# The forget gates' chain ahead of the value casts, and two NSA output tiles that take the last pair of heads behind the others, in a two-layer hybrid attention trunk

## The chip, the cores and the metric

The kernel runs on one core of one Trainium2 chip. The metric is the device time of one execution in microseconds (us). The engines are TensorE (PE; its weight loads are shown as PEld), VectorE (DVE), ScalarE (ACT), GpSimd (POOL) and SyncE (SP, which here only issues transfers). Each engine runs its own list of instructions in order; semaphores hold an instruction until what it reads has been written and what it overwrites has been read.

## The reference: what is computed

The input is x, 512 tokens by 1024 channels, float32. Each of two layers computes, cut to what matters here:

```python
h = rmsnorm(x, norm_mix)
q_a, k_a, v_a, f_a, q_b, kv_b, g_b, gate_a, gate_b = split(h @ w_in)
log_f = log_sigmoid(f_a + b_forget)                  # 8 forgetting heads (FoX)
c = cumsum(log_f)                                    # over the tokens
s = q_a @ k_a.T / 8 + c[:, None] - c[None, :]        # causal
y_a = (softmax(s) @ v_a) @ w_o_fox
# NSA: 8 query heads, 2 key/value heads; three branches
# (compressed, selected, sliding window) with partial rotary embedding
o_n = g[..., 0:1]*o_c + g[..., 1:2]*o_s + g[..., 2:3]*o_w     # g = sigmoid(g_b)
y_b = o_n @ w_o_nsa
mixed = sigmoid(gate_a)*y_a + sigmoid(gate_b)*y_b
x = x + mixed @ w_out
x = x + square(relu(rmsnorm(x, norm_mlp) @ w_up)) @ w_down
```

A final rmsnorm follows the second layer. The forget chain makes c, a running sum of the logarithms of the forget gates. At the end of the attention the change touches o_n and its product with w_o_nsa.

## The kernel before, in words

The whole trunk is one stream of work on one core. The state is held with channels on the partitions and the 512 tokens along the free axis. A float32 product is made from rounded pieces: each operand is split into a high part (fp32r) and the remainder, and for every block of 128 channels PE runs three matmuls of 512 columns: high by high (L243), high weight by low data (L244), low weight by high data (L245). The weights arrive as raw float32 by a transfer on SP (L201); `convert` rounds them on ACT (L217, tile wh) and subtracts on DVE (L218, tile wl). There are two buffers each for raw, wh and wl, and a raw buffer is free for the next load when the split has read it.

The order of every engine's instructions is not the source order alone: the kernel is written against a scheduler that places each instruction of a whole stage by its readiness and priority, so a small edit of the source can move instructions elsewhere on several engines. The source's order still says which result an instruction needs and which buffer it takes.

A layer (`Body.layer`) goes through these steps:

- `token_proj` makes the FoX values, four blocks of 128 tokens, in the PSUM banks S, S, PT, PT. `rstd` makes the reciprocal norm: rc, with one column for each block of tokens, and R, the same spread over the partitions.
- A second `token_proj` of 288 columns makes, for each block b, g2[b]: 256 columns of NSA values, 8 of the forget gates, 24 of NSA's branch gates. They lie in the banks mm, mm, O, O. Its matmuls are the lines L357 to L359.
- For each block the kernel then makes z (forget logits, DVE L884), th (tanh of the branch gates, ACT L886), and the high and low part of the NSA values VN (ACT L887, DVE L888). The gates follow (DVE L891, L893).
- CRS, the table of cosines and sines for the rotary embedding, is loaded (L895, on SP, 512 KB) and multiplied by R in two instructions on POOL (L897). It is one tile for both layers.
- `forget` (L783 to L808) turns the 128x32 logits into log sigmoid by a chain of small instructions, one on ACT (L789, exp) and the others on DVE (L788 to L799, among them a polynomial in six steps, L796). Ten matmuls of 128 columns (L805, L806) then make the running sum over the tokens in bank S.
- The projections of q, k and the gates (`block`, one bank and 24 matmuls each), FoX attention, NSA attention. Both attentions have the same shape on the engines: scores on PE, exp on ACT, a reciprocal and normalization on DVE (FoX L449 and L454, NSA L562 and L566), transposes on PE (FoX L464, NSA L579), casts and splits of those, products with the values.
- The end of each NSA pair of heads (`after`, four of them in a layer): four matmuls for the compressed branch (L962), then for each half of the 128 output rows a copy out of PSUM (ACT L969) and an addition (DVE L970), and the split into oh and ol (`out_pair`, ACT L495, DVE L496).
- The output projection of NSA, eight tiles m, two for each 128x1024 weight tile w. `half(1, m, w)` runs twelve matmuls: for each of the four pairs k (the entries of yb) the three kinds L243, L244, L245. The last pair's oh and ol are the newest data they need. Then the gate is applied (DVE L1039, L1040), and `mix` splits the sum (L1030, L1031) for w_out. The MLP follows.

PSUM has eight banks of 128x512; a tag such as "mm" or "S" names a pair of banks that take turns, so a matmul that begins a new tile waits until the bank's last reader is done.

Of the kernel before, what the change touches and what calls it, by code (L numbers as in the profile page):

```python
# [14 lines left out]
OP = mybir.AluOpType  # L15
# [4 lines left out]
T = 512  # L20
KT = D // 128
NB = T // 128
# [10 lines left out]
OFF, N_SMALL = {}, 0  # L33
# [104 lines left out]
def run(*gens):  # L138
    for g in gens:
        for _ in g:  # L140
            pass


class Body:
# [705 lines left out]
    def layer(self, l, u):  # L850
        nc, a = self.nc, self.a
# [10 lines left out]
        R, rc = self.rstd(self.acc, ("O", "O"), wait=g, R=self.R)  # L862
        run(g)
        small = self.small
        g2 = [self.p(t) for t in ("mm", "mm", "O", "O")]
        g = self.token_proj([[a["wg2"][l, c].rearrange("p j m -> p (j m)")] for c in range(4)], 288, g2, u)
        VF = []
        for b in range(NB):
# [4 lines left out]
                                           op0=OP.mult, op1=OP.subtract)  # L873
# [2 lines left out]
        VN = self.t("vn", [128, NB, 4, 128], F32R)  # L876
        z = self.t("z", [128, NB, 8])
        th = self.t("th", [128, NB, 24])
        rch = self.t("s4", [128, NB], name="rch")
        nc.vector.tensor_scalar(rch, rc, 0.5, None, op0=OP.mult)  # L880
        for b in range(NB):
            pv = g2[b][:, :256].rearrange("p (h d) -> p h d", h=4)
            r = rc[:, b:b + 1]
            nc.vector.scalar_tensor_tensor(z[:, b], g2[b][:, 256:264], r, small[:, OFF["bf"]:OFF["bf"] + 8],  # L884
                                           op0=OP.mult, op1=OP.add)
            nc.scalar.activation(th[:, b], g2[b][:, 264:288], AF.Tanh, scale=rch[:, b:b + 1])  # L886
            nc.scalar.activation(VN[:, b, :, :64], pv, AF.Copy, scale=r)  # L887
            nc.vector.scalar_tensor_tensor(VN[:, b, :, 64:], pv, r, VN[:, b, :, :64].bitcast(F32),  # L888
                                           op0=OP.mult, op1=OP.subtract)
        self.gates = gt = self.t("gates", [128, NB, 3, 8])  # L890
        nc.vector.tensor_scalar(gt, th.rearrange("p b (h c) -> p b c h", c=3), 0.5, 0.5, op0=OP.mult, op1=OP.add)  # L891
        for b in range(NB):
            nc.vector.tensor_scalar(gt[:, b, 0], gt[:, b, 0], self.const("rowv")[:, b:b + 1], None, op0=OP.mult)  # L893
        self.CRS = self.t("crs", [128, 2, T])
        nc.sync.dma_start(self.CRS, a["rope"])  # L895
        for i in range(2):
            nc.gpsimd.tensor_tensor(self.CRS[:, i], self.CRS[:, i], R, op=OP.mult)  # L897
        self.forget(z.rearrange("p b h -> p (b h)"))

        st, hl = {}, []  # L900

# [52 lines left out]
        def nsa_pair(p):  # L954

            hk = p // 2
            O = [None]

            def after(O):
                for e in range(2):  # L960
                    for bank in range(2):
                        nc.tensor.matmul(O[:, bank, e], self.vz[:, hk, e],  # L962
                                         self.pc[hk][p % 2][:, bank * 256:(bank + 1) * 256], start=False, stop=e == 1)
                o = self.t("zz", [128, T], name="o")
                t = self.t("tmp", [128, T])
                half = lambda x: x.rearrange("p (b c) -> p b c", b=2)
                for e in range(2):
                    s, f = slice(64 * e, 64 * e + 64), slice(64 * (1 - e), 64 * (1 - e) + 64)
                    nc.scalar.copy(half(t[s]), O[f, :, e])  # L969
                    nc.vector.tensor_add(half(o[s]), O[s, :, e], half(t[s]))  # L970
                st["ob", p] = self.out_pair(o)

            ready = (lambda: ("qb", p) in st and "ks" in st and "kw" in st, lambda: hk in self.pc)

            def unit(br, e):
                return dict(br=br, e=e, p=p, hk=hk, O=O, after=after, ready=ready[br], kk=lambda: KK[hk],
                            q=lambda: st["qb", p][:, e], v=lambda b: VN[:, b, 2 * br + hk],
                            gate=lambda: gt[:, :, 1 + br, 2 * p + e],
                            steps=(self.pair_scores, self.pair_transposes, self.pair_values))
            u = [unit(br, e) for br in range(2) for e in range(2)]  # L980
            for i in range(4):
                u[i]["other"], u[i]["second"] = u[(i + 2) % 4], u[i | 1]
            return u

        def half(kind, m, w):

            xs = ya if kind == 0 else yb
            ps = self.p("mm")
            yield from self.gemm(ps, w, 4 * (m % 2), xs, ks=4)
            st["y"] = ps  # L990
# [30 lines left out]
        yb = [st["ob", p] for p in range(4)]  # L1021
# [4 lines left out]
        def mix():  # L1026
            y = MA[len(mixed) // 2][:, len(mixed) % 2]
            h = self.t("oh", [128, T], F32R)
            lo = self.t("ol", [128, T], F32R)
            nc.scalar.activation(h, y, AF.Copy, scale=0.5)  # L1030
            nc.vector.scalar_tensor_tensor(lo, y, 0.5, h.bitcast(F32), op0=OP.mult, op1=OP.subtract)  # L1031
            mixed.append((h, lo))

        for m in range(8):
            if m % 2 == 0:
                w = self.weights(a["wo"][l, 1, m // 2].rearrange("p i c -> p (i c)"))
            run(half(1, m, w))
            t, y = st["gb", m], MA[m // 2][:, m % 2]
            nc.vector.scalar_tensor_tensor(t, t, 1.0, st["y"], op0=OP.add, op1=OP.mult)  # L1039
            nc.vector.tensor_add(y, y, t)  # L1040
            if m % 2:
                mix()
# [9 lines left out]
        for m in range(8):  # L1052
            ps = self.bank()
            w = self.weights(a["wout"][l, m].rearrange("p k c -> p (k c)"))
# [439 lines left out]
```

## Time and profile before

| | |
|---|---|
| median of three runs | 1522.34 us (1522.2 to 1523.99) |
| the profiled execution | 1523.61 us, of which the profile's span is 1521.8 us |
| granted clock of PE, mean | 0.997 |
| PE busy | 1507.1 us, 99% of the span |
| DVE, ACT, POOL busy | 1097.7, 810.0, 191.1 us |
| transfers | 188.81 MB, 124 GB/s over the span |

A row of the timeline reads: start in us, length in us, engine and line, operation, output<-inputs with the tile names of the program, shape, how many instructions the row stands for, and in brackets the idle time of that engine just before, with what ended it. The length is from the start of an instruction until its result is there; a matmul of 512 columns has a length of 0.39, but the next can start sooner, since PE is a pipeline. A row with x2 or x4 stands for several neighbours. SPq marks the issuing of a transfer, not the transfer. The list of waits reads: engine, output tile and line, the releaser, then idle us in total, how often, and the longest.

### The profile page before, as it was taken

The numbers are of one execution on the slowest core, as the hardware profiler recorded it, in microseconds if no ns is written. First come the engines' busy times: TensorE is split into PE (matmuls) and PEld (weight loads), VectorE is DVE, ScalarE is ACT, GpSimd is POOL, SyncE is SP. The second block draws the span as 40 slices with busy tenths as digits, with TensorE's granted clock in tenths as the row PEclk, the third lists the DMA queues.
The fourth block names the chain that finished last, engine by engine and source line by source line (L and its number), as shares of the span: only waits on it lengthen the run. The fifth ranks groups of instructions, "written<-read, shape, count | busy, mean of one in ns | idle before, by whom it ended". The sixth has DMA issues, their size and how long they took to land.

```text
span 1521.8 us, 21129 instructions
## 1 busy us (share of the span) xinstructions
PE 1507.1 (99%) x7688; PEld 1262.0 (83%) x7688; DVE 1097.7 (72%) x2094; ACT 810.0 (53%) x1532; POOL 191.1 (13%) x184
## 2 busy tenths in 40 slices
PE   9999999999999999999999999999999999999997
PEld 8888888887888888888888788888888888888897
DVE  5678978777478777775646799787674979766762
ACT  6365656554454655555435556555544636555553
POOL 4000000000300222112310000000012003222122
PEclk9999999999999999999999999999999999999998
DMA  7555522227334455422546552322462255544121
GB/s 259 160 154 143 147 70 84 70 70 225 114 97 145 134 146 138 144 78 64 176 148 168 159 137 84 93 70 68 134 181 97 96 152 147 151 130 140 50 84 56
DMA packets 67575, 188.81 MB, mean 124 GB/s; under 512 B 8560, under 2 KB 9968, under 8 KB 67472
## 3 DMA queue, kind: packets, MB, share of 16 engines
q1 hardware_dynamic: 56672, 168.31, 35.8%
q0 software_dynamic: 6912, 12.59, 4.9%
q10 hardware_dynamic: 3888, 6.58, 1.2%
q8 instruction: 60, 0.98, 0.3%
q14 instruction: 43, 0.35, 0.1%
HBM read 147.53 MB, written 4.19 MB: 100 GB/s over the span
## 4 chain that ended last, share of the span: by engine, by line
PE 92%; DVE 4%; ACT 3%; issue 1%; DMA 0%; DVEq 0%; ACTq 0%
PE ps_mm L243 13%; PE ps_mm L244 12%; PE ps_mm L245 12%; PE ps_PT L244 3%; PE ps_PT L243 3%; PE ps_PT L245 3%; PE ps_O L1388 3%; PE ps_S L1388 3%; PE ps_mm L1388 3%; PE ps_O L605 2%; PE ps_PT L579 2%; PE ps_PT L1388 2%; PE ps_S L243 2%; PE ps_S L244 2%; PE ps_S L245 2%; PE ps_S L554 2%
## 5 line engine op out<-in xcount | busy, mean ns | idle before, releaser
L217 ACT CAST wh<-raw 128x1024 fp32r<-128x1024 f32 (+2 forms) x187 | 192.3, 1029 | 282.8 <-issue 90.6
L218 DVE TENSOR_TENSOR wl<-raw,wh 128x1024 fp32r<-128x1024 f32 (+2 forms) x187 | 225.5, 1206 | 48.9 <-ACT wh L217 48.1
L243 PE MATMUL ps_mm<-uh,wh 128*128 128x512 f32 x512 | 205.2, 401 | 0.0
L245 PE MATMUL ps_mm<-uh,wl 128*128 128x512 f32 x512 | 202.1, 395 | 0.1
L244 PE MATMUL ps_mm<-ul,wh 128*128 128x512 f32 x512 | 201.8, 394 | 0.0
L243 PE MATMUL ps_mm<-oh,wh 128*128 128x512 f32 (+1 forms) x316 | 123.0, 390 | 2.1 <-ACT oh L495 1.7
L245 PE MATMUL ps_mm<-oh,wl 128*128 128x512 f32 (+1 forms) x316 | 122.1, 386 | 0.0
L244 PE MATMUL ps_mm<-ol,wh 128*128 128x512 f32 (+1 forms) x316 | 122.0, 386 | 0.0
L1378 DVE TENSOR_TENSOR sl<-raw,sh 128x512 fp32r<-128x512 f32 x120 | 96.7, 814 | 31.6 <-ACT sh L1377 30.8
L245 PEld LDWEIGHTS ps_mm<-uh,wl 128*128 128x128 f32 x512 | 96.3, 188 | 20.1 <-DVE wl L218 0.3
L243 PEld LDWEIGHTS ps_mm<-uh,wh 128*128 128x128 f32 x512 | 96.7, 189 | 19.4 <-issue 1.2
L244 PEld LDWEIGHTS ps_mm<-ul,wh 128*128 128x128 f32 x512 | 96.4, 188 | 16.6
L1351 POOL DMA_DIRECT2D raw<-raw x24 | 21.2, 885 | 703.1 <-DMA x<-xs 241.6
L583 ACT CAST pth<-ps_PT 128x384 fp32r<-128x384 f32 (+1 forms) x96 | 48.9, 511 | 66.2 <-PE ps_PT L579 66.0
L541 DVE CUSTOM_DVE_ANT_0 E<-ps_S,ct 128x384 f32<-128x384 f32 (+3 forms) x112 | 57.4, 515 | 31.5 <-PE ps_S L554 30.6
L542 ACT ACTIVATE E<-E,tiny 128x384 f32<-128x384 f32 (+3 forms) x112 | 65.6, 586 | 20.4 <-DVE tiny L541 20.1
L1377 ACT CAST sh<-raw 128x512 fp32r<-128x512 f32 x120 | 72.8, 618 | 4.3 <-PE ps_mm L1388 2.0
L243 PEld LDWEIGHTS ps_mm<-oh,wh 128*128 128x128 f32 x316 | 59.3, 188 | 14.6 <-ACT oh L495 2.6
L245 PEld LDWEIGHTS ps_mm<-oh,wl 128*128 128x128 f32 x316 | 59.5, 188 | 12.2
L244 PEld LDWEIGHTS ps_mm<-ol,wh 128*128 128x128 f32 x316 | 59.5, 188 | 11.3 <-DVE ol L496 0.9
L243 PE MATMUL ps_PT<-oh,wh 128*128 128x512 f32 x172 | 67.7, 393 | 0.0
L245 PE MATMUL ps_PT<-oh,wl 128*128 128x512 f32 x172 | 67.3, 391 | 0.0
(441 smaller groups left out, 3927.6 us busy)
## 6 DMA issues: line engine op xcount, KB each, us to landing
raw<-wb SPq DMA_DIRECT2D x64, 512.0 KB
raw<-wup SPq DMA_DIRECT2D x64, 512.0 KB
raw<-wd SPq DMA_DIRECT2D x48, 512.0 KB
raw<-raw POOLq DMA_DIRECT2D x48, 256.0 KB, 3.5
w<-w SPq DMA_DIRECT2D x32, 256.0 KB
kda<-hla SPq DMA_DIRECT2D x32, 256.0 KB
q2a<-hla SPq DMA_DIRECT2D x64, 128.0 KB
raw<-wo SPq DMA_DIRECT2D x16, 512.0 KB
```

The lines of the kernel that those rows point to most:

```text
L217: nc.scalar.copy(h[:, :n], raw[:, :n])
L218: nc.vector.tensor_tensor(lo[:, :n], raw[:, :n], h[:, :n].bitcast(F32), op=OP.subtract)
L243: mm(ps, h[:, c], xh, start=start and i == 0, stop=False)
L244: mm(ps, h[:, c], xl, start=False, stop=False)
L245: mm(ps, lo[:, c], xh, start=False, stop=stop and i == ks - 1)
L541: nc.vector.tensor_tensor_reduce(e, ps, self.mask[:, T - n:], -1.0, BIG, OP.add, OP.min, mx)
L542: nc.scalar.activation(e, e, AF.Exp, bias=mx, scale=-1.0, accum_out=un["sm"][:, i:i + 1])
L554: nc.tensor.matmul(ps[:, :n], qs, kk[:, br, f, :n], start=f == 0, stop=f == 1)
L583: nc.scalar.copy(h[:, e, :n], ps[:, :n])
L1377: nc.scalar.copy(h, src)
L1378: nc.vector.tensor_tensor(lo, src, h.bitcast(F32), op=OP.subtract)
L1388: mm = lambda o, w, x, **kw: self.nc.tensor.matmul(o, w, x, skip_group_check=True, **kw)
```

## The change

Four edits, the first two in both layers at the start of the attention, the last two in both layers at the end of NSA.

- z of all four blocks and the whole forget chain are written ahead of th, VN, the gates and the load of CRS; before they came behind these.
- A copy of one column (128x1) from rc into CRS on POOL is written ahead of the load of CRS. The load overwrites that column, so it waits for the copy, and the copy waits for rc.
- The temporary of a pair's end is one tile for each half instead of one for the pair.
- The first two output tiles, m = 0 and 1, share the weight tile w. They now take one bank of each of the tags mm and S, run pairs 0 to 2 for both tiles and then the last pair for both. The other six are as before.

In the profile of the changed kernel the lines below the forget call are renumbered (L884 becomes L880, L897 becomes L900, L962 becomes L964, L969 and L970 become L971 and L972, L1039 becomes L1050).

```diff
@@ layer: behind the second token_proj
         th = self.t("th", [128, NB, 24])
+        for b in range(NB):
+            nc.vector.scalar_tensor_tensor(z[:, b], g2[b][:, 256:264], rc[:, b:b + 1], small[:, OFF["bf"]:OFF["bf"] + 8],
+                                           op0=OP.mult, op1=OP.add)
+        self.forget(z.rearrange("p b h -> p (b h)"))
         rch = self.t("s4", [128, NB], name="rch")
         nc.vector.tensor_scalar(rch, rc, 0.5, None, op0=OP.mult)
         for b in range(NB):
             pv = g2[b][:, :256].rearrange("p (h d) -> p h d", h=4)
             r = rc[:, b:b + 1]
-            nc.vector.scalar_tensor_tensor(z[:, b], g2[b][:, 256:264], r, small[:, OFF["bf"]:OFF["bf"] + 8],
-                                           op0=OP.mult, op1=OP.add)
             nc.scalar.activation(th[:, b], g2[b][:, 264:288], AF.Tanh, scale=rch[:, b:b + 1])
...
         self.CRS = self.t("crs", [128, 2, T])
+        nc.gpsimd.tensor_copy(self.CRS[:, 0, :1], rc[:, :1])
         nc.sync.dma_start(self.CRS, a["rope"])
         for i in range(2):
             nc.gpsimd.tensor_tensor(self.CRS[:, i], self.CRS[:, i], R, op=OP.mult)
-        self.forget(z.rearrange("p b h -> p (b h)"))
@@ the end of an NSA pair
                 o = self.t("zz", [128, T], name="o")
-                t = self.t("tmp", [128, T])
                 half = lambda x: x.rearrange("p (b c) -> p b c", b=2)
                 for e in range(2):
                     s, f = slice(64 * e, 64 * e + 64), slice(64 * (1 - e), 64 * (1 - e) + 64)
+                    t = self.t("tmp", [128, T])
                     nc.scalar.copy(half(t[s]), O[f, :, e])
@@ the output projection of NSA
         for m in range(8):
             if m % 2 == 0:
                 w = self.weights(a["wo"][l, 1, m // 2].rearrange("p i c -> p (i c)"))
-            run(half(1, m, w))
+            if m == 0:
+
+                first = [self.p(tag) for tag in ("mm", "S")]
+                for k, ks in ((0, 3), (3, 1)):
+                    for i, ps in enumerate(first):
+                        run(self.gemm(ps, w, 4 * i + k, yb[k:], ks=ks, start=k == 0, stop=k == 3))
+            if m < 2:
+                st["y"] = first[m]
+            else:
+                run(half(1, m, w))
             t, y = st["gb", m], MA[m // 2][:, m % 2]
```

## The prediction

> **What bounds the kernel now.** I read the engine shares first, then the list of waits of the matmul engine, then the timeline around each wait, and last how the change orders each engine's instructions.
>
> ```profile
> span 1521.8 us, 21129 instructions
> PE 1507.1 (99%) x7688; PEld 1262.0 (83%) x7688; DVE 1097.7 (72%) x2094; ACT 810.0 (53%) x1532; POOL 191.1 (13%) x184
> ```
> PE is busy for 1507.1 of 1521.8 us. The change takes no matmul away, so all it can win lies in the remaining 14.7 us and in gaps too short to be listed as idle.
>
> ```profile
> PE ps_mm L243 <- ACT oh L495: 1.7, 2, 0.9
> PE ps_S L806 <- issue: 0.6, 1, 0.6
> PE ps_mm L358 <- DVE wl L218: 0.3, 1, 0.3
> PE ps_S L806 <- DVE tiny L799: 0.3, 1, 0.3
> ```
> These are the waits that the edits touch: the last NSA pair (twice), the forget matmuls (once in each layer) and one weight split. Shown idle time sums to 2.9 us, but a pipelined matmul hides part of a stall, so below I compare starts with the pitch.
>
> **NSA's output tiles (both layers).**
>
> ```profile
> 351.06 0.58 ACT L969 COPY tmp<-ps_O 64x512 f32<-64x512 f32 x1 [2.95 <-PE ps_O L962]
> ...
> 352.39 0.58 ACT L969 COPY tmp<-ps_O 64x512 f32<-64x512 f32 x1 [0.75 <-DVE o L970]
> ...
> 352.91 0.39 PE L244 MATMUL ps_mm<-ol,wh 128*128 128x512 f32 x1
> 353.00 0.69 DVE L970 TENSOR_TENSOR o<-ps_O,tmp 64x512 f32<-64x512 f32 x1 [0.65 <-ACT tmp L969]
> 353.14 0.39 PE L245 MATMUL ps_mm<-oh,wl 128*128 128x512 f32 x1
> 353.73 0.62 ACT L495 CAST oh<-o 128x512 fp32r<-128x512 f32 x1 [0.76 <-DVE o L970]
> ...
> 354.40 0.73 PE L243 MATMUL ps_mm<-oh,wh 128*128 128x512 f32 x2 [0.87 <-ACT oh L495]
> 355.12 0.50 PE L244 MATMUL ps_mm<-ol,wh 128*128 128x512 f32 x1
> ...
> 356.17 0.40 PE L243 MATMUL ps_mm<-oh,wh 128*128 128x512 f32 x1
> ```
> Matmuls of 512 columns start 0.23 apart (352.91 to 353.14; 0.227 over longer stretches). From 353.14 to 356.17 seven start (two in the x2 row, then 355.12 and three more), which at 0.227 is 1.59; it took 3.03, so the stall is 1.44 us, in two places: on oh (1.03) and on ol and the refill behind it.
>
> ```profile
> 1102.07 0.39 PE L245 MATMUL ps_mm<-oh,wl 128*128 128x512 f32 x1
> ...
> 1103.33 0.73 PE L243 MATMUL ps_mm<-oh,wh 128*128 128x512 f32 x2 [0.87 <-ACT oh L495]
> ...
> 1105.09 0.39 PE L243 MATMUL ps_mm<-oh,wh 128*128 128x512 f32 x1
> ```
> Layer 1 is the same: 3.02 - 1.59 = 1.43.
>
> The separate tile for each half buys nothing here: in the new order the second copy still waits for the first half's add, as the row at 352.39 does, so the chain from 351.06 to oh at 354.35 (353.73 + 0.62), and to ol behind it, keeps its length. Nor is the written order of m = 0 and 1 new: before already ran three k of both tiles ahead of the wait. What is new is that the second bank ("S") frees a bank for m = 2: five of its matmuls now stand ahead of the first that needs oh, and a sixth between that pair and the first that needs ol. Five cover 5 x 0.227 = 1.14 against 1.03, the sixth the rest. The weights of m = 2 are split well before, ahead of the row at 351.06 on DVE's order. I take 1.40 per layer, 2.8 in all. Lower bound 1.14 per layer (the five alone), upper 1.44; the margin at oh is only 0.1.
>
> **The forget chain (both layers).**
>
> ```profile
> 44.64 0.22 DVE L884 SCALAR_TENSOR_TENSOR tiny<-ps_O,tiny,small 128x8 f32<-128x8 f32 x1
> ...
> 53.21 0.39 PE L243 MATMUL ps_PT<-uh,wh 128*128 128x512 f32 x1
> 53.95 0.19 DVE L799 SCALAR_TENSOR_TENSOR tiny<-tiny 128x32 f32<-128x32 f32 x1
> ...
> 54.24 0.38 PE L806 MATMUL ps_S<-ct,tiny 128*8 128x128 f32 x2 [0.64 <-issue]
> ...
> 802.96 0.39 PE L243 MATMUL ps_PT<-uh,wh 128*128 128x512 f32 x1
> ...
> 803.39 0.19 DVE L799 SCALAR_TENSOR_TENSOR tiny<-tiny 128x32 f32<-128x32 f32 x1
> ...
> 803.64 0.39 PE L806 MATMUL ps_S<-ct,tiny 128*8 128x128 f32 x2 [0.29 <-DVE tiny L799]
> ```
> Stalls: 54.24 - 53.21 - 0.23 = 0.80 and 803.64 - 802.96 - 0.23 = 0.45. The same small DVE instructions run. Their first starts about 2.2 us earlier (near 45.3, right behind the z of 44.64 and the last z, which no longer follows a weight split and value casts); 0.8 of that is given back, because that split of 1.2 us now falls inside the chain. So timed by the starts of its rows, L799 comes near 52.55 in layer 0, 1.4 earlier. The scheduler spends most of it: the ten forget matmuls stand five matmuls (1.14) earlier on PE. Left are 1.4 - 1.14 = 0.3 in layer 0 and about 0.4 in layer 1, 0.7 together; bounds 0 (the chain gains only 1.14) and 1.25 (both stalls gone). If it gained nothing, the five lost covers would cost 1.14 per layer; the z rows that move exclude that.
>
> **The rope load and the POOL products.** The new copy into CRS waits for rc and makes the load wait for the copy; on SP it moves behind three w1 loads and the last wg2 load.
>
> ```profile
> 27.97 0.43 SPq L895 DMA_DIRECT2D crs<-rope  x1
> ...
> 30.79 0.92 SPq L638 DMA_DIRECT2D w<-w  x2
> ...
> 34.10 2.55 POOL L897 TENSOR_TENSOR crs<-crs,ct 128x512 f32<-128x512 f32 x2 [9.57 <-DMA crs<-rope]
> ...
> 36.03 1.24 DVE L218 TENSOR_TENSOR wl<-raw,wh 128x576 fp32r<-128x576 f32 x1 [0.75 <-ACT wh L217]
> ...
> 36.72 0.29 PE L357 MATMUL ps_mm<-wh,uh 128*128 128x288 f32 x1
> ...
> 37.33 0.40 PE L358 MATMUL ps_mm<-wl,uh 128*128 128x288 f32 x1 [0.31 <-DVE wl L218]
> ...
> 37.62 0.76 DVE L218 TENSOR_TENSOR wl<-raw,wh 128x576 fp32r<-128x576 f32 x1 [0.35 <-ACT wh L217]
> ```
> The same split took 1.24 beside the POOL products and 0.76 alone; PE lost 37.33 - 36.72 - 0.13 = 0.48. The load now issues near 31.7 as the last of its batch.
>
> ```profile
> 36.00:36.50 0.50, 0.50 (x6) 0.50 (x5) 0.47 (x1) 0.00 (x1) 0.50 (x1) 1.00 0.05 16
> ```
> This row of the table by stretches has the DMA engines 5% busy (the last column but one) from 36.0 on, so the batch ends there; with a landing delay of about 1 us I put the products near 36.9: behind the first split and onto the second, whose first use comes 24 matmuls of 0.133 after the first's slot, near 40.1; held by both products it ends at 40.2. Gain 0.45; bounds +0.48 and -1.9 (products that start just ahead of 36.03 hold the split by their whole 2.55 rather than 0.62). The copy itself and its place on SP cost nothing: SP issued nothing from 31.71 until a weight load that waits for the 36.03 split. In layer 1 the list of waits shows no such split.
>
> The Trainium skill (GPSIMD Engine Reference, Instruction dispatch) speaks against the copy: the first call of a freshly loaded GpSimd function pays an instruction load of about 6 us, and no copy has run there before. By that the products would land near 42 us and the sum would be about 0.5 worse by my estimate. No run so far shows a POOL copy.
>
> **What the scheduler moves besides.** PE's order changes at two more places.
>
> ```profile
> 71.10 1.28 DVE L454 TENSOR_SCALAR E<-E,tiny 128x128 f32<-128x128 f32 x4
> ...
> 71.62 0.41 PE L464 MATMUL ps_PT<-tiny,E 128*128 128x128 f32 x2
> ...
> 73.01 0.34 SPq L201 DMA_DIRECT2D raw<-wb  x1
> ...
> 74.01 0.48 PE L243 MATMUL ps_mm<-uh,wh 128*128 128x512 f32 x1
> ...
> 77.48 1.05 ACT L217 CAST wh<-raw 128x1024 fp32r<-128x1024 f32 x1 [2.21 <-DMA raw<-wb]
> ...
> 80.10 0.50 PE L245 MATMUL ps_mm<-uh,wl 128*128 128x512 f32 x1
> ```
> First FoX heads, layer 0: the weight load of 73.01 moves up to about 65, and its cast (1.05) and split (1.2) now stand ahead of the last exp (ACT) and of the four normalizations (DVE, 1.28), whose first starts near 73.2 instead of 71.10. PE pulls six matmuls (1.36) ahead of the transposes, which so begin at 73.45 for a slot at 72.98, and each next one waits for its block: the matmul of 74.01 comes near 74.7, +0.7. Back come 0.35 around 80.10, where before waited for that split. Net +0.35; bounds 0 and 0.9.
>
> ```profile
> 233.82 1.22 DVE L218 TENSOR_TENSOR wl<-raw,wh 128x1024 fp32r<-128x1024 f32 x1
> ```
> Second NSA pair, both layers: this split moves ahead of the first half's add, about 4 us up, and the transposes of the pair follow sooner. By starts of the rows DVE is just in time at each of them: 0, bounds -0.3 (gain) and +0.75 per layer (if each instruction took its whole row's duration before the next started).
>
> **Sum.** -2.8 - 0.7 - 0.45 + 0.35 + 0 = -3.6 us. The profiled execution took 1523.61 (span 1521.8 and 1.8 around it), so 1520.0 of that kind; it lies 1.27 above the median 1522.34 of runs from 1522.2 to 1523.99, so 1518.7 as a median.
>
> **Rivals.**
> 1. Only part works: the margins at the NSA end fail (1.14 each) and the forget chain keeps its stall (0), while the rest holds: -2.3 - 0.45 + 0.35 = -2.4, 1519.9. For it: a margin of 0.1 us. Against it: the covers are whole matmuls with operands long ready.
> 2. The POOL products start just ahead of the first split, because the load, though last, lands sooner than I think: -3.6 + 0.45 + 1.9 = -1.25, 1521.1. For it: the products need to come only 0.9 sooner than 36.9. By the copy's own cost or the skill's 6 us they come later instead, at most onto another split.
> 3. The other side, slower: the moved weight load is late. It now stands ahead of the last exp on ACT, in order, so every us that it lands after 70.7 delays the whole first FoX softmax and PE by as much. Load to cast took 77.48 - 73.01 = 4.5; from 65 that is 69.5. With -3.6 from the rest, it ends slower only if the load lands after 74.3, taking twice as long; at 76 the time would be 1524.0.
> 4. The change does not do what it says: the separate half tiles certainly don't shorten the chain. If the extra m = 2 matmuls did not cover either, only the forget and POOL gains less the FoX loss would be left: -0.8, 1521.5.
>
> **How the numbers follow.** The forecast 0.48, rival 1 0.22, rival 2 0.12, rival 3 0.06, rival 4 0.12. 0.2% is 3.0 us, about what a measurement tells from no change, so the forecast lies 0.6 beyond the bound: most of its weight and a little of rival 1 counts as faster (0.50), the others as the same (0.44); slower by more than 0.2% needs most of rival 3 (0.06). Range: with all gains at their best (-2.88 - 1.25 - 0.48 and no losses, -4.6) 1517.7, upward to rival 4, 1521.5; at both ends 0.8 more, half the spread of the runs shown above (1522.2 to 1523.99), since one median of few runs is compared: 1516.9 to 1522.3.
>
> **What would show it.** In the changed profile: no wait of L243 on oh (over 0.1) near 354 and 1103, else the cover is short; L806 waits near 0.45 and 0.05; the POOL products start after 36.1 and the split takes 0.76; the first L464 starts near 73.4, later than 71.62; no new waits near 237 to 244. The prediction is wrong if a weight cast or a DVE split that was moved up becomes a new wait in PE's list, or if the first POOL copy takes microseconds.

## The result, and the profile after

The changed kernel takes 1520.25 us (median of 17 runs, 1518.78 to 1522.41); the kernel before, run beside it, 1522.79 us (17 runs, 1521.57 to 1524.34). The ratio is 0.9983 with a 95% interval of 0.9976 to 0.999: 2.5 us faster, where 3.6 were forecast. The profiled execution took 1520.41 us, with a span of 1518.6 and a mean granted clock of 0.997, as before.

The profile page's engine shares, and the list of waits of PE (releaser, idle us in total, times, longest):

```profile
span 1518.6 us, 21145 instructions
PE 1504.6 (99%) x7688; PEld 1261.6 (83%) x7688; DVE 1096.3 (72%) x2094; ACT 811.1 (53%) x1532; POOL 191.5 (13%) x186
```

```profile
PE ps_S L359 <- DVE ul L266: 0.9, 1, 0.9
...
PE ps_mm L358 <- DVE wl L218: 0.8, 1, 0.8
...
PE ps_S L806 <- issue: 0.2, 1, 0.2
...
PE ps_mm L245 <- DVE wl L218: 0.2, 1, 0.2
```

The wait on oh is gone from the list, and of the forget waits 0.2 is left. But the wait on the split (L358) has grown from 0.3 to 0.8, and two waits are new: 0.9 on L266, in the norm at the very start, where none of the four edits lies, and 0.2 on a split (L245), at 834 us.

The end of NSA in layer 0, then layer 1, by the timeline:

```profile
353.23 0.39 PE L243 MATMUL ps_mm<-oh,wh 128*128 128x512 f32 x1
...
353.59 0.62 ACT L495 CAST oh<-o 128x512 fp32r<-128x512 f32 x1 [0.76 <-DVE o L972]
...
354.13 0.39 PE L244 MATMUL ps_mm<-ol,wh 128*128 128x512 f32 x1
...
354.26 0.19 PEld L243 LDWEIGHTS ps_mm<-oh,wh 128*128 128x128 f32 x1 [0.17 <-ACT oh L495]
354.36 0.40 PE L243 MATMUL ps_mm<-oh,wh 128*128 128x512 f32 x1
...
355.07 0.41 PE L244 MATMUL ps_mm<-ol,wh 128*128 128x512 f32 x1
...
1100.80 0.39 PE L243 MATMUL ps_mm<-oh,wh 128*128 128x512 f32 x1
...
1101.94 0.40 PE L243 MATMUL ps_mm<-oh,wh 128*128 128x512 f32 x1
```

From 353.23 to 354.13 the five matmuls of m = 2 fill the place of the stall, and the first that needs oh starts at 354.36, exactly one pitch behind them. oh was ready at 354.21 (353.59 + 0.62): the margin of 0.1 held. Layer 1 repeats it: 1100.80 + 5 x 0.227 = 1101.94.

The forget matmuls, in both layers:

```profile
52.93 0.39 PE L244 MATMUL ps_PT<-ul,wh 128*128 128x512 f32 x1
53.25 0.18 DVE L799 SCALAR_TENSOR_TENSOR tiny<-tiny 128x32 f32<-128x32 f32 x1
53.53 0.38 PE L806 MATMUL ps_S<-ct,tiny 128*8 128x128 f32 x2 [0.21 <-issue]
...
800.47 0.39 PE L244 MATMUL ps_PT<-ul,wh 128*128 128x512 f32 x1
800.48 0.18 DVE L799 SCALAR_TENSOR_TENSOR tiny<-tiny 128x32 f32<-128x32 f32 x1
800.79 0.38 PE L806 MATMUL ps_S<-ct,tiny 128*8 128x128 f32 x2
```

The stall is 53.53 - 52.93 - 0.23 = 0.37 in layer 0 (before 0.80) and 0.09 in layer 1 (before 0.45).

The rope load and the products on POOL (a row with x2 runs over both instructions and the idle time between them):

```profile
31.52 0.18 POOL L897 COPY crs<-tiny 128x1 f32<-128x1 f32 x1 [8.28 <-DVE tiny L309]
...
31.73 0.33 SPq L898 DMA_DIRECT2D crs<-rope  x1
...
36.24 3.04 POOL L900 TENSOR_TENSOR crs<-crs,ct 128x512 f32<-128x512 f32 x2 [4.54 <-DMA crs<-rope]
...
36.42 3.47 DVE L218 TENSOR_TENSOR wl<-raw,wh 128x576 fp32r<-128x576 f32 x2 [0.74 <-ACT wh L217]
...
38.19 0.40 PE L358 MATMUL ps_mm<-wl,uh 128*128 128x288 f32 x1 [0.79 <-DVE wl L218]
```

The copy takes 0.18 us and the load issues when it was forecast. But the products start at 36.24, 0.18 ahead of the first split, not at 36.9 behind it. Taken one by one, the first product runs from 36.24 to 37.52 and the first split from 36.42 to 38.13, 0.61 past the end of that product; the second product, which meets that split, takes 1.80 instead of 1.30.

To find where the rest of the time lies I put each matmul of a profile beside the matmul of the same number in PE's list of the kernel before (all have 7688), and took the difference of their starts. What that difference gains or loses over a stage is the price of the stage (us, minus is faster; us of the kernel before name the stage). The runs are those of the next section.

| stage | after | after_again | after_wait | after_late | after_no_b | after_no_c | a_only | b_only | b_wait | c_only | d_only | bank_only | a_bank |
|---|---|---|---|---|---|---|---|---|---|---|---|---|---|
| 18 to 22, first norm | +0.89 | +0.92 | +0.24 | +1.08 | -0.01 | +0.90 | +0.01 | +0.92 | 0.00 | +0.01 | -0.01 | +0.17 | 0.00 |
| 34 to 39, split beside POOL | +0.47 | +0.63 | +0.62 | -0.48 | +0.28 | +0.46 | -0.46 | -0.47 | -0.48 | +0.11 | -0.05 | -0.48 | +0.13 |
| 39 to 52, next split | 0.00 | 0.00 | 0.00 | +0.49 | 0.00 | 0.00 | 0.00 | 0.00 | 0.00 | 0.00 | 0.00 | 0.00 | 0.00 |
| 52 to 57.5, forget, layer 0 | -0.42 | -0.40 | -0.69 | -0.41 | -0.40 | -0.39 | -0.37 | -0.01 | -0.29 | +0.02 | 0.00 | 0.00 | -0.41 |
| 70 to 81.5, first FoX heads | -0.56 | +1.22 | +0.05 | -0.53 | -0.02 | -0.41 | -0.04 | -0.25 | +1.01 | 0.00 | -0.02 | -0.01 | -0.07 |
| 84 to 200 | +0.23 | +0.62 | +0.26 | +0.37 | -0.06 | +0.59 | +0.04 | +0.42 | +0.57 | -0.05 | -0.06 | -0.05 | 0.00 |
| 200 to 352.5, NSA pairs, layer 0 | -0.23 | -0.27 | -0.23 | -0.28 | -0.26 | +0.04 | +0.04 | +0.04 | -0.03 | -0.26 | +0.01 | +0.03 | +0.02 |
| 352.5 to 357.5, NSA end, layer 0 | -1.41 | -1.40 | -1.41 | -1.41 | -1.41 | -1.40 | -0.02 | -0.03 | -0.04 | -0.04 | -1.41 | -1.40 | -1.41 |
| 530 to 536, MLP | +0.38 | +0.87 | +0.13 | -0.13 | +0.08 | +0.60 | +1.45 | +0.86 | -0.05 | -0.09 | -0.13 | +0.08 | +0.70 |
| 800 to 807, forget, layer 1 | -0.35 | -0.35 | -0.35 | -0.35 | -0.35 | -0.35 | -0.35 | 0.00 | 0.00 | 0.00 | 0.00 | 0.00 | -0.35 |
| 825 to 840 | +0.48 | +0.40 | +0.02 | +0.41 | +0.04 | +0.04 | +0.03 | 0.00 | +0.06 | -0.01 | -0.01 | 0.00 | +0.07 |
| 975 to 1040, NSA pairs, layer 1 | -0.24 | -0.23 | -0.28 | -0.27 | -0.27 | -0.05 | -0.07 | -0.05 | -0.03 | -0.27 | -0.05 | -0.05 | -0.02 |
| 1101.5 to 1106.5, NSA end, layer 1 | -1.35 | -1.34 | -1.37 | -1.34 | -1.35 | -1.35 | +0.01 | -0.02 | +0.02 | -0.01 | -1.35 | -1.35 | -1.35 |

A stage's price in this table is read against one profile of the kernel before, so a figure that is the same in every kernel with an edit, and nought without it, belongs to that edit; one that changes between two executions of the same kernel (530 to 536) does not. Nor does one that changes between kernels whose instructions are alike up to there: the six kernels without the copy into CRS run the instructions of the kernel before until 41 us, in the same order on PE, DVE, ACT and POOL, and the split at 34 to 39 costs them from -0.48 to +0.28. One run of b_only, 2127.35 us, stands apart from its other ten, whose median is 1524.58.

### The profile page after: what moved, and what is told of

Its sections match the earlier page's. It is cut to its first block, busy times and chain, and to the rows that moved or that the text cites. A ratio compares the mean times of both kernels' runs of the same rounds, so it can differ in the third digit from the quotient of the medians.

```text
span 1518.6 us, 21145 instructions
## 1 busy us (share of the span) xinstructions
PE 1504.6 (99%) x7688; PEld 1261.6 (83%) x7688; DVE 1096.3 (72%) x2094; ACT 811.1 (53%) x1532; POOL 191.5 (13%) x186
## 4 chain that ended last, share of the span: by engine, by line
PE 89%; DVE 6%; ACT 3%; DMA 1%; issue 1%; POOL 0%; DVEq 0%; ACTq 0%; POOLq 0%; SPq 0%
PE ps_mm L243 12%; PE ps_mm L245 12%; PE ps_mm L244 12%; PE ps_PT L243 4%; PE ps_PT L245 4%; PE ps_PT L244 4%; PE ps_O L1399 3%; PE ps_S L1399 3%; PE ps_mm L1399 3%; PE ps_S L243 2%; PE ps_S L245 2%; PE ps_S L244 2%; PE ps_O L605 2%; PE ps_PT L579 2%; PE ps_PT L1399 2%; PE ps_O L243 2%
## 5 line engine op out<-in xcount | busy, mean ns | idle before, releaser
L217 ACT CAST wh<-raw 128x1024 fp32r<-128x1024 f32 (+2 forms) x187 | 192.3, 1029 | 281.0 <-issue 86.6
L245 PE MATMUL ps_mm<-uh,wl 128*128 128x512 f32 x512 | 201.8, 394 | 0.2 <-DVE wl L218 0.2
L245 PE MATMUL ps_mm<-oh,wl 128*128 128x512 f32 (+1 forms) x308 | 119.0, 386 | 0.0
L244 PE MATMUL ps_mm<-ol,wh 128*128 128x512 f32 (+1 forms) x308 | 118.7, 385 | 0.0
L245 PEld LDWEIGHTS ps_mm<-uh,wl 128*128 128x128 f32 x512 | 96.2, 188 | 20.2 <-DVE wl L218 0.3
L245 PEld LDWEIGHTS ps_mm<-oh,wl 128*128 128x128 f32 x308 | 58.0, 188 | 12.0
L245 PE MATMUL ps_PT<-oh,wl 128*128 128x512 f32 x172 | 67.3, 391 | 0.0
L244 PE MATMUL ps_PT<-ol,wh 128*128 128x512 f32 x172 | 67.1, 390 | 0.0
```

The costliest lines, as they stand in the source:

```text
L217: nc.scalar.copy(h[:, :n], raw[:, :n])
L244: mm(ps, h[:, c], xl, start=False, stop=False)
L245: mm(ps, lo[:, c], xh, start=False, stop=stop and i == ks - 1)
```

## The experiments

Each median stands beside the kernel before on the same chip: 1523.02 us (33 runs) for the first four, 1523.18 (32 runs) for the second four, 1523.10 (30 runs) for the last four. Interval and ratio are against that.

**The four edits alone.** Their diffs are those of the change, one at a time: a_only has z and the forget chain ahead, b_only the POOL copy into CRS, c_only the temporary for each half, d_only the two output tiles in mm and S.

> The kernel before with the first edit alone: z and the forget chain ahead of th, VN, gates and the load of CRS. Theory 1 (the edits act separately, as the shifts between the two traces read): the ten forget matmuls come 0.4 us sooner in each layer, the wait in front of the first of them falls from 0.80 to about 0.4 in layer 0 and from 0.45 to about 0.05 in layer 1, nothing else moves, -0.8 us in all. Theory 2 (the edit costs elsewhere, since gates and value casts come later): the forget gain is there but a new wait of 0.3 us or more stands behind it, in the FoX part of either layer (about 70 to 80 or about 834 us), and the sum is within 0.3 us of zero.

> The kernel before with the second edit alone: the 128x1 copy on POOL ahead of the load of CRS. Theory 1: the load goes out near 31.5 instead of 27.97, lands near 36, the two POOL products start within 0.4 us of the third weight split of the 288-column product, and the wait for that split grows from 0.48 to about 0.95 us (+0.5); the weight load that moves up on SP brings the first FoX heads 0.5 us back; sum about 0. Theory 2 (the collision in the changed kernel was a chance of that execution): the products start behind the split, the wait is gone (-0.45), and with the FoX part the sum is about -1.0 us.

> The kernel before with the third edit alone: one temporary for each half of a pair's end. Theory 1: the second copy waits for the first half's addition with or without it, so the waits on oh near 354 and 1103 stay at 0.87 us shown; the second NSA pair is reordered (transposes 1 to 1.5 us sooner) at no gain; 0 us, within 0.3. Theory 2 (the tile does break the chain): the waits on oh shrink by the 0.6 us of a copy, -1.2 us over both layers.

> The kernel before with the fourth edit alone: m = 0 and 1 in banks mm and S, the last pair behind the others. Theory 1: it is the whole gain at the NSA ends, 1.35 to 1.4 us per layer, no wait of L243 on oh is left near 354 and 1103, -2.7 us in all. Theory 2 (it needs the separate half tiles with it): about half of it.

| kernel | median, us | runs from | to | ratio | 95% interval |
|---|---|---|---|---|---|
| a_only | 1522.22 | 1521.14 | 1523.46 | 0.9996 | 0.9987 to 1.0005 |
| b_only | 1524.74 | 1522.83 | 2127.35 | 1.0010 | 1.0001 to 1.0019 |
| c_only | 1522.63 | 1521.51 | 1525.15 | 1.0001 | 0.9992 to 1.0009 |
| d_only | 1520.26 | 1519.25 | 1521.06 | 0.9982 | 0.9973 to 0.9990 |

The last edit alone is as fast as the whole change, 2.8 us below the kernel before. The POOL copy alone is slower, by 1.5 us, which neither of its theories had: its products start 0.30 behind the split, and the split's wait is gone.

```profile
36.65 0.76 DVE L218 TENSOR_TENSOR wl<-raw,wh 128x576 fp32r<-128x576 f32 x1 [0.75 <-ACT wh L217]
...
36.95 3.37 POOL L898 TENSOR_TENSOR crs<-crs,ct 128x512 f32<-128x512 f32 x2 [5.02 <-DMA crs<-rope]
```

But the first norm costs 0.92, the stretch from 84 to 200 us 0.42, and in this execution the MLP 0.86. The forget chain's two gains of 0.37 and 0.35 stand in the table by stage, but 0.7 us is less than the medians tell apart.

**The bank alone.** In d_only two things change: the bank of m = 1, and the order written out for m = 0 and 1. This kernel has the first alone:

```diff
-        def half(kind, m, w):
+        def half(kind, m, w, tag="mm"):
             xs = ya if kind == 0 else yb
-            ps = self.p("mm")
+            ps = self.p(tag)
...
-            run(half(1, m, w))
+            run(half(1, m, w, "S" if m == 1 else "mm"))
```

> The kernel before with one word of the fourth edit: m = 1 takes a bank of the tag S, while m = 0 and 1 are written one after the other as before. Theory 1 (the free bank for m = 2 is what lets five of its matmuls stand ahead of the wait; the written order of the pairs is the scheduler's own work anyway): the same -2.7 us as the whole fourth edit, no wait on oh left. Theory 2 (the written order matters): the waits on oh stay at 0.87 us shown, within 0.3 us of the kernel before.

It took 1520.26 us (1519.13 to 1520.67), ratio 0.9979 (0.9970 to 0.9988), with -1.40 and -1.35 at the two ends of NSA:

```profile
352.37 0.39 PE L243 MATMUL ps_mm<-oh,wh 128*128 128x512 f32 x1
...
352.73 0.62 ACT L495 CAST oh<-o 128x512 fp32r<-128x512 f32 x1 [0.76 <-DVE o L970]
...
353.50 0.40 PE L243 MATMUL ps_mm<-oh,wh 128*128 128x512 f32 x1
```

Here, too, five matmuls stand between 352.37 and 353.50. The word "S" is the whole gain of the fourth edit; the order written out by hand adds nothing to what the scheduler did: PE, DVE, ACT and POOL run the same instructions in the same order in the profiles of d_only and bank_only.

**The changed kernel without one edit, and with a later copy.** after_no_b leaves the copy out; after_no_c has one temporary for the pair. after_late lets the copy wait for a later tile, so that the load issues later:

```diff
-        nc.gpsimd.tensor_copy(self.CRS[:, 0, :1], rc[:, :1])
+        nc.gpsimd.tensor_copy(self.CRS[:, 0, :1], VF[3][:, 0, 64:65].bitcast(F32))
```

> The changed kernel without the copy on POOL: the load of CRS goes out early as in the kernel before. Theory 1: the wait on the split falls back to about 0.48 us shown as 0.3 (-0.5 against the changed kernel), the first FoX heads lose their 0.5 us again; sum within 0.3 us of the changed kernel. Theory 2 (the copy is the cause of the FoX order's gain only, and the split's wait is chance): +0.5 us against the changed kernel.

> The changed kernel with one temporary for a pair's end, as before. Theory 1 (the separate half tiles buy nothing, and reorder the second NSA pair at no gain): within 0.3 us of the changed kernel, and no wait on oh near 354 and 1103. Theory 2: the waits on oh come back in part (0.3 us or more shown each).

> The changed kernel with one difference: the copy that holds back the load of CRS reads the last FoX value tile instead of rc, so the load goes out about 4 us later, near 36, and the POOL products start near 39 to 40, behind the splits of the 288-column product and ahead of the next (near 42). Theory 1 (the products hold the DVE split that they meet, 0.95 us of wait in the changed kernel): the wait of L358 on the split goes, about -0.9 us against the changed kernel, 1519.3 us. Theory 2 (the split is late for another reason): the wait of 0.8 us shown stays. Theory 3: the products meet the next split, and a wait of 0.5 us or more appears near 43 to 45 us instead.

| kernel | median, us | runs from | to | ratio | 95% interval |
|---|---|---|---|---|---|
| after_no_b | 1519.47 | 1518.61 | 1522.07 | 0.9978 | 0.9969 to 0.9987 |
| after_no_c | 1521.58 | 1519.40 | 1523.26 | 0.9990 | 0.9981 to 0.9999 |
| after_late | 1520.95 | 1519.40 | 1522.18 | 0.9985 | 0.9976 to 0.9994 |

Without the copy the kernel is no slower, and the 0.9 at 18 to 22 us is gone; all four kernels so far with the copy have it. The split's wait near 37 is there without the copy too (+0.28 against the kernel before), so this run doesn't show that the copy makes it. after_late clears the split near 37 (-0.48), as its theory on the products said, and pays the same 0.49 at the next one, as the rival said:

```profile
39.78 2.54 POOL L900 TENSOR_TENSOR crs<-crs,ct 128x512 f32<-128x512 f32 x2 [3.70 <-DMA crs<-rope]
...
43.29 1.23 DVE L218 TENSOR_TENSOR wl<-raw,wh 128x1024 fp32r<-128x1024 f32 x1 [4.35 <-ACT wh L217]
...
44.57 0.50 PE L245 MATMUL ps_PT<-uh,wl 128*128 128x512 f32 x1 [0.20 <-DVE wl L218]
```

So after_late shows a displacement, not a saving. c_only and the five others of the table with the third edit gain 0.23 to 0.28 between 200 and 352.5 us and 0.23 to 0.28 between 975 and 1040, the kernels without it next to nothing (-0.03 to +0.04, -0.07 to -0.02): 0.5 us in both layers, a gain that the medians of c_only and after_no_c are too coarse to show. The profile has no wait of PE there with the edit or without it; from 225 to 280 us the steps from a matmul to the next transpose are 19 and take 5.22 us in the kernel before, 18 and 4.71 in c_only, so it is the new order that seems to pay. after_no_c was expected within 0.3 of the changed kernel and came out 1.6 below the kernel before instead of 2.5; the intervals overlap, and what of that is the third edit stays open.

**The 0.9 us ahead of all edits.** What follows is the timeline of the first norm. In the kernel before:

```profile
18.31 1.29 POOL L284 TENSOR_TENSOR acc<-sq,acc 128x512 f32<-128x512 f32 x1 [0.74 <-ACT sq L274]
...
19.63 0.63 ACT L274 ACTIVATE sq<-x 128x512 f32<-128x512 f32 x1 [1.40 <-POOL acc L284]
19.63 0.75 DVE L266 SCALAR_TENSOR_TENSOR ul<-x,tiny,uh 128x512 fp32r<-128x512 f32 x1 [1.28 <-POOL acc L284]
...
20.34 1.30 POOL L284 TENSOR_TENSOR acc<-sq,acc 128x512 f32<-128x512 f32 x1 [0.74 <-ACT sq L274]
```

In the changed kernel:

```profile
17.73 2.66 POOL L284 TENSOR_TENSOR acc<-sq,acc 128x512 f32<-128x512 f32 x2 [0.74 <-ACT sq L274]
...
19.07 1.88 DVE L266 SCALAR_TENSOR_TENSOR ul<-x,tiny,uh 128x512 fp32r<-128x512 f32 x1 [3.56 <-POOL acc L284]
...
21.00 0.50 PE L359 MATMUL ps_S<-wh,ul 128*128 128x512 f32 x1 [0.91 <-DVE ul L266]
```

Before, the sixth square (19.63) waits for the POOL product of 18.31, and DVE's L266 runs in the gap that this leaves on POOL. In the changed kernel that square no longer waits, two products run back to back, and L266 takes 1.88 instead of 0.75, until the second product has ended and 0.56 us more. The Trainium skill (SBUF — State Buffer, "SBUF: two separate sides") has a rule for this: a DVE instruction with two inputs in SBUF and a GpSimd instruction that reads SBUF take a port that they share as an exclusive lock for the whole instruction, and the other blocks. L266 fits it: the products end at 17.73 + 2.66 = 20.39 and L266 at 20.95, as if it had been held until then. It doesn't take two products. Earlier in the changed kernel a single one does the same, and the lag is 0.56 again (14.95 and 15.51):

```profile
13.16 1.79 POOL L284 TENSOR_TENSOR acc<-sq,acc 128x512 f32<-128x512 f32 x1 [2.99 <-ACT sq L274]
...
13.73 1.78 DVE L266 SCALAR_TENSOR_TENSOR ul<-x,tiny,uh 128x512 fp32r<-128x512 f32 x1
```

So it matters whether a product runs as L266 begins, and without the square's wait the next product starts at once at 19.11. By the records L266 begins 0.04 ahead of that product, so which of the two came first can't be read from them.

That the missing wait is the cause, and not something else of the copy, was tried by giving the wait back: a copy of one column on POOL from the running sum into the sixth square's tile, which the square must then wait for.

```diff
         s = self.t("tmp", [128, T], name="sq")[:, :n]
+        self.nsq = getattr(self, "nsq", 0) + 1
+        if self.nsq == 6:
+            nc.gpsimd.tensor_copy(s[:, :1], acc[0][:, :1])
         nc.scalar.activation(s, x, AF.Square)
```

after_wait is the changed kernel with this, b_wait is b_only with it; after_again is the changed kernel as it is.

> The changed kernel, and a copy of one column (128x1) on POOL from the sum acc into the sixth square's tile ahead of that square (L274), so that this square again waits for the POOL product of the square before it, as it does in the kernel before. The orders of PE are those of the changed kernel. Theory 1 (the 0.9 us that every kernel with the copy into CRS loses at 19 to 21 us comes from this missing wait: two POOL products run back to back and hold DVE's L266): POOL L284 comes in single rows of 1.3 again, L266 near 19 takes 0.75 and not 1.88, PE's list has no L359 <- DVE ul of 0.9, PE at 22 us is 0.9 earlier than in the changed kernel, and the whole comes 0.7 to 1.0 below the changed kernel (near -3.4 against before, ratio 0.9978). Theory 2 (the loss has another cause in the copy into CRS, such as where tiles lie): the wait of PE at 21 stays, and the time is that of the changed kernel (ratio 0.9983).

> The kernel before with the copy into CRS alone, and the same added wait of the sixth square. Theory 1: 0.9 us of the 1.5 that the copy alone cost goes away, ratio near 1.0004, and the stage at 19 to 21 us takes as long as in the kernel before; what is left is the split near 37 and whatever POOL does behind. Theory 2: as the copy alone, ratio 1.001.

> The changed kernel as it is, beside the three others on the same chip, for a second profiled execution. Theory 1 (the wait of 0.9 on L266 at 21 us and the 0.44 at 835 belong to the order of the instructions): both are there again. Theory 1 on the split near 37: the 0.8 wait of L358 depends on when the rope load's last bytes land and can be gone or there in this execution. Rival: all three come again alike, then the split's wait is the order's too. Time: ratio 0.9983 against before, as measured.

| kernel | median, us | runs from | to | ratio | 95% interval |
|---|---|---|---|---|---|
| after_wait | 1518.88 | 1517.32 | 1520.38 | 0.9970 | 0.9960 to 0.9980 |
| after_again | 1520.34 | 1519.08 | 1523.32 | 0.9980 | 0.9972 to 0.9989 |
| b_wait | 1523.07 | 1522.04 | 1524.12 | 0.9999 | 0.9990 to 1.0008 |

after_wait, the same stretch:

```profile
17.85 1.28 POOL L287 TENSOR_TENSOR acc<-sq,acc 128x512 f32<-128x512 f32 x1 [0.74 <-ACT sq L277]
...
19.17 0.76 DVE L266 SCALAR_TENSOR_TENSOR ul<-x,tiny,uh 128x512 fp32r<-128x512 f32 x1 [1.27 <-POOL acc L287]
19.20 0.18 POOL L276 COPY sq<-acc 128x1 f32<-128x1 f32 x1
...
19.41 0.63 ACT L277 ACTIVATE sq<-x 128x512 f32<-128x512 f32 x1 [1.64 <-POOL sq L276]
...
20.13 1.29 POOL L287 TENSOR_TENSOR acc<-sq,acc 128x512 f32<-128x512 f32 x1 [0.74 <-ACT sq L277]
```

L266 is back at 0.76, and the wait of PE at 21 us is gone; the stage costs 0.24 instead of 0.9 (a smaller wait of 0.26 near 17.95 us, on the L266 before, is in this execution), and in b_wait 0.00 instead of 0.92. Theory 1 holds for the stage: an added instruction and an added wait take 0.65 and 0.92 us away there. after_wait has the lowest median of all kernels here, 1.46 us below after_again on the same chip; the two intervals overlap. Not all of that is this stage: from 825 to 840 us after_wait loses 0.02 instead of 0.40, and from 52 to 57.5 it is 0.29 better, as b_wait is against b_only (-0.29, -0.01), though neither has a new order there; the cast (L217) ahead of the chain starts sooner after idle time that the profile puts down to nothing. Why the square lost its wait is argued, not shown: in the record of the changed kernel the sixth square waits for no semaphore, in the kernel before for one of POOL, while the order of the instructions up to there is unchanged. The copy makes CRS begin to be used later, so the placing of the temporaries in memory is the likely cause.

after_again has all three waits again (+0.92, +0.63, +0.40), as its rival said: in the changed kernel the split's wait didn't come and go.

**The two parts that gain.** a_bank has the forget chain ahead (as a_only) and the bank S for m = 1 (as bank_only), and nothing else.

> The two parts that gained, alone: the forget chain ahead of the value casts, and bank S for m = 1 with the written order of before; no copy into CRS, one temporary for a pair. Theory 1 (the parts add): -0.75 - 2.9 = -3.6 us against before, ratio 0.9976, below the changed kernel by about 1 us. Rival (what one part gains at 55 or 355 us is taken back by a later stage once the other is there, as in the changed kernel at 835): -2.5, ratio 0.9983, no better than the changed kernel.

It took 1520.30 us (1518.75 to 1521.26), ratio 0.9980 (0.9971 to 0.9989). By stage both parts give what they give alone (-0.41, -1.41, -0.35, -1.35: -3.5), and of the stages behind them only the wait at 530 to 536 us takes 0.7 back in this execution. By the median it is 2.8 below the kernel before, not 3.6. after_no_b, which differs from it by the third edit (0.5 by stage) and the written order, came to -3.7. Differences of 0.8 between medians of eleven runs stay open here.

**The first FoX heads: a transfer that sets the time.** The same kernel paid -0.56 in one profiled execution and +1.22 in the other. The changed kernel, then after_again, then b_wait:

```profile
65.33 0.58 SPq L201 DMA_DIRECT2D raw<-wb  x1
...
70.38 0.19 ACT L445 ACTIVATION_READ_ACCUMULATOR E<-E,tiny 128x1 f32 x1
70.47 1.04 ACT L217 CAST wh<-raw 128x1024 fp32r<-128x1024 f32 x1
...
73.44 0.44 PE L464 MATMUL ps_PT<-tiny,E 128*128 128x128 f32 x2
```

```profile
65.32 0.58 SPq L201 DMA_DIRECT2D raw<-wb  x1
...
72.21 1.05 ACT L217 CAST wh<-raw 128x1024 fp32r<-128x1024 f32 x1 [1.64 <-DMA raw<-wb]
...
75.14 0.50 PE L464 MATMUL ps_PT<-tiny,E 128*128 128x128 f32 x2 [1.53 <-DVE E L454]
```

```profile
63.72 0.58 SPq L201 DMA_DIRECT2D raw<-wb  x1
...
70.44 1.05 ACT L217 CAST wh<-raw 128x1024 fp32r<-128x1024 f32 x1 [1.44 <-PE ps_mm L245]
...
73.28 0.59 PE L467 MATMUL ps_PT<-tiny,E 128*128 128x128 f32 x2 [1.25 <-DVE E L457]
```

The copy into CRS moves this weight load, its cast and its split ahead of the last exp and of the normalizations (b_only has the move, a_only, c_only and bank_only don't). In the changed kernel the cast at 70.47 follows ACT's own work (the row of 70.38) without idle time, so the load was there by then. The trace holds the landing itself: it records 16 parts of the load, and the last of them came at 69.59 in the changed kernel, 4.3 us after the issue, and at 72.13 in after_again, 6.8 us after it. In b_wait, where the load was issued 1.6 us earlier, it came at 70.36; the wait that the row of 70.44 puts down to a matmul ended with the load too. In after_again and b_wait 15 of the 16 parts were there by 69.86 and 67.70, so a single part sets the time; why it is late isn't shown. In the four other kernels with the copy the last part came at 69.49 (after_late), 70.30 (after_wait), 70.39 (b_only) and 70.80 (after_no_c).

So what PE had won by then can be lost at the transposes: b_wait came 1.1 us ahead to 70 us and started L467 at 73.28, only 0.16 ahead of the changed kernel, which came 0.4 late. And where the load lands 2.5 later, as in after_again, all of PE waits for it.

## Why the prediction was right and wrong, step by step

The forecast was 1518.7 us within 1516.9 to 1522.3, and the kernel took 1520.25: inside the range, 1.5 above the forecast. Of that 0.45 is the kernel before, which in 17 runs came to 1522.79 and not to 1522.34; the change itself gave 2.5 of the 3.6. That it lies in the range is in part luck: the split and the first norm came out 0.9 us each worse than told, and against them the profiled execution gained 0.9 more at the first FoX heads than told, where the other execution lost 0.9 more. Two steps were right, and carry the whole gain.

**NSA's output tiles: right.** 1.41 and 1.35 measured, 1.40 each forecast, with the cause as told: the bank, not the order (bank_only) and not the half tiles (-0.04 at that stage in c_only). The margin of 0.1 held in every kernel with the bank, so rival 1 had no case here, and rival 4 neither. That the separate half tiles buy nothing is right for the pair's end alone; between the pairs they bring 0.25 in each layer.

**Forget chain: right.** 0.42 and 0.35 in the table against 0.3 and 0.4.

**The rope load: wrong in sign.** The step took 36.9 for the start of the products, from a batch of transfers that ended near 36.0 before. In the changed kernel they start at 36.24, 0.18 ahead of the first split, which is the condition of rival 2, and the split waits: +0.47 in place of -0.45. The 1.9 of the bound was too much, since the split is held by one product and not by both: it ends 0.61 us after the first (37.52, 38.13), and the second waits for it. The split of the kernel before ends 0.61 after the product that it met, too (36.66, 37.27). In b_only and b_wait the products come behind the split's start (36.95 against 36.65, 36.31 against 35.64), and there the stage gives the forecast 0.47. But a_only and bank_only give 0.46 and 0.48 without the copy, because there the split begins as a product is about to end (35.39 against 35.55, 35.53 against 35.67), and after_no_b loses 0.28: the wait of 0.48 in the profile of before was itself one draw out of several, and no gain of the copy is shown in this stage. The four executions with the copy behind rc and the forget edit all have the wait (+0.46 to +0.63), the two with the copy alone don't; whether that is more than chance stays open. The mechanism, products that hold a split, was the right one, and its term was decided by a few tenths of landing time that a trace of another kernel could not give. The sentence "The copy itself and its place on SP cost nothing" was the larger error: the copy's own 0.18 us is indeed nothing, and no load of 6 us appears (the Trainium skill's rule, GPSIMD Engine Reference, Instruction dispatch, does not show on this copy), but with it a wait at 19 us is gone, and that cost 0.9 there. I had looked at the order ahead of 30 us, which is unchanged, and not at which instructions wait.

**First FoX heads: the step was a term where it had to be a race.** Forecast was +0.35 (0 to 0.9), measured -0.56 and +1.22 in two executions. In the changed kernel L464 started at 73.44 for a forecast of 73.45, but by another way: PE came 0.43 late, so its slot was 73.41 and not 72.98, the delay cost it nothing, and the 0.6 behind (the forecast's "0.35 around 80.10") were all gain. Rival 3 had named the mechanism, a moved load that every us after 70.7 pays for. Its landing at 69.5, from a constant 4.5 us, was right for this execution (69.59) and for after_late (69.49); in the five others with the copy the load landed 0.7 to 2.5 us later, and twice that cost PE about 1 us. Between 84 and 200 us the next load comes late as well, and 0.2 to 0.6 are given back in every kernel with the copy.

**Second NSA pair: right within its bounds.** Forecast 0 (-0.3 to +0.75); the third edit gives -0.23 to -0.28 in each layer, at the best end of the bounds.

**What no step had.** Beside the 0.9 of the first norm, 0.48 at 825 to 840 us in layer 1: DVE runs the addition L378 ahead of the split that PE needs. It comes in after, after_again and after_late, whose order it is, and goes in after_wait, where PE's order is the same and DVE runs the split ahead of L378 again; it isn't in after_no_c and after_no_b, so neither the copy nor the third edit makes it alone. The wait at 530 to 536 us is in kernels of all kinds and was 0.38 and 0.87 in two executions of the changed kernel; it is charged to no edit. The profile puts it down to a low part (ol) made on POOL, which stands there behind the issue of a transfer; why that issue comes at different times stays open.

The account by stage of the changed kernel's profile: NSA ends -2.76, forget -0.77, NSA pairs -0.47, first FoX heads and what follows to 200 us -0.33; against them the first norm +0.89, the split +0.47, layer 1's split +0.48: -2.5. The medians differ by 2.5 as well, but the two profiled spans by 3.2 (1521.8 and 1518.6): to the -2.5 come +0.4 at 530 to 536 us and -1.1 from stretches that the table doesn't list, -0.6 of it ahead of 18 us, where both kernels run the same instructions.

## What to carry to other kernels

Here a tile that could begin in a free bank was worth 1.4 us at each place, and an order written by hand nothing: look for which buffer the next ready work lacks. When a schedule is made by a program, compare the waits of the two kernels as well as the orders, from the first instruction on; a wait that disappears can let two engines collide, and what PE gains ahead of a late transfer can be lost again at that transfer. A wait in one profile of the kernel before may be a draw of that execution: look at it in a second one before a gain is built on it. A landing time read from the kernel before is good for a range, not for a term, once the step turns on less than a microsecond.

## What the runs showed of the hardware

- A DVE instruction of two inputs in SBUF (L266, 128x512) takes 0.75 us alone and 1.78 to 1.88 where a POOL product with inputs in SBUF runs as it begins; it then ends 0.56 us after that product. The split of 128x576 takes 0.76 alone and ends 0.61 after the product that it meets (37.52, 38.13 in the changed kernel), and the product that follows takes 1.80 instead of 1.30.
- A load of 512 KB landed 4.3 us after its issue in one execution and 6.8 in another of the same kernel (65.33 to 69.59, 65.32 to 72.13); in the slow one 15 of its 16 parts were there at 69.86.
- The first copy of the program on POOL took 0.18 us.
